# Low parts of weights and rotary products of a two-block model: from GpSimd to VectorE

## Chip, cores and metric

The kernel runs on one core of a Trainium2 chip. The metric is the device time of one execution in microseconds (us), the median of several runs. The engines are called as in the profile: PE is TensorE (PEld its weight loads), DVE VectorE, ACT ScalarE, POOL GpSimd, SP SyncE.

## What is computed

The reference runs two transformer blocks of two layers each on 512 tokens of 1024 features, in float32. The first block (differential attention, a recurrent branch, a gated feed-forward part) is not touched by the change. The second one is:

```python
def second_block(x, mem, positions, ...):
    for l in range(DEPTH):
        mix = hybrid_mixer(x, positions, w_in[l], conv_w[l], rel_bias[l], w_mix_out[l])
        x = layer_norm(ALPHA * x + mix, ln1_g[l], ln1_b[l])
        cross = memory_cross_attention(x, mem, w_mq[l], w_mkv[l], w_mo[l])
        x = layer_norm(ALPHA * x + cross, ln2_g[l], ln2_b[l])
        ff = squared_relu_mlp(x, w_ff1[l], w_ff2[l])
        x = layer_norm(ALPHA * x + ff, ln3_g[l], ln3_b[l])
    return x
```

`hybrid_mixer` projects x once and splits the result for three paths: a short gated convolution; an attention in which each query attends to the 128 keys that an indexer scores highest (8 small heads, a relu, a weighted sum, then a top-k); and an attention in chunks of 64 tokens over a band, with a relative bias. Queries and keys of the second path and of the indexer are turned by rotary tables:

```python
    rot = jnp.concatenate([x1 * cos - x2 * sin, x2 * cos + x1 * sin], axis=-1)
```

## The kernel before

Features lie on the partitions. Every large product is made of three float32r matmuls (`mm3`): high part of the weight by high part of x, high by low, low by high. A weight of 128 output features (128x1024 for all input features) is loaded by `weight` (L83): SP starts the load of `wraw` (L88), ACT rounds it to the high part `whi` (L90), and VectorE or, where `eng` says so, GpSimd subtracts that to get the low part `wlo` (L92). Each of the three tiles has three buffers, so the next weights are made while PE works on this one. A product over 512 tokens takes 24 matmuls.

```python
        (eng or nc.vector).tensor_sub(lo[:, :kt], raw[:, :kt], f(hi[:, :kt]))
```

`POOLW` (seven numbers) sets who makes the low parts in the second block's mixer: the first three numbers stand for the three weights of each pair of heads of the chunk attention (`C`), the fourth for the queries (`Q`), the last three for the convolution (`conv`). Before, the first and the third of each three are GpSimd's: 10 of them per layer, between weights that DVE makes.

`rope` (L643 to L654) turns a projection p: DVE swaps rows into `rt` (L650) and multiplies p by the cosines into `ru` (L651), `rt` is multiplied by the sines (L652), DVE adds the two (L653). It is called for the keys (two products of 64 rows each time), the indexer's queries and the queries.

`Norm.close` makes the last products before a norm over half the tokens at a time, and between them loads up to three weights of the next part ahead. The second one (`i == 1`) has its low part made by GpSimd. That happens at three places: before the first feed-forward products in both layers, and before the second layer's mixer.

The mixer's order is written in `STEPS2`: `H`, `I` input products, `i2`, `i1`, `i3` the indexer for three tiles of queries with 384, 256 and 512 keys (128x384, 128x256 and 128x512 sums called `isc`), `Q` queries, `C` and `A` chunk attention, `v` convolution, `d` attention to the chosen keys, `p` a part of the top-k. In the indexer (L876 to L888) PE makes the scores of a head into one of two banks `sc` (L880), ACT applies the relu into one of two buffers `p` (L882), DVE adds the weighted result to `isc` (L887 the first head, L884 the others). The top-k (L895 MAX8, L896 MATCH_REPLACE, L899 at its end) runs on DVE in pieces among the attentions. An attention adds its bias on DVE (L814), takes the exponential on ACT, the reciprocal on DVE (L817) and scales on ACT (L821); PE then transposes (L827) and multiplies.

The program is not run in the order in which it is written: a list scheduler of the framework sets, from its own costs, the order of each engine's queue. Each engine then works through its queue in order. A change of engine for one kind of operation so also changes the order of others.

Of the kernel before, what the change touches and what calls it, by code (L numbers as in the profile page):

```python
# [25 lines left out]
# columns of the first block's packed per-feature parameters  # L26
G_MIX, G_FFN, QG, KG, SUB, CW, CB, BRG, BIG, LRU, RECG, LAM = 0, 8, 16, 17, 18, 19, 35, 39, 43, 47, 51, 55
N_PAR1 = 59
# columns of the packed shape constants
# [5 lines left out]
# columns of the second block's packed per-feature parameters  # L35
# [11 lines left out]
def both_blocks(ctx: ExitStack, tc: tile.TileContext, xT, cst, par1, w1in, w1out, w1gu, w1dn, wgate,  # L47
# [6 lines left out]
    EARLY = 4  # tiles of features that the norms' first centre is taken from  # L54
# [7 lines left out]
    # ---- residual (features on partitions) and constants  # L62
# [4 lines left out]
    # the operand of most products: 8 tiles in two parts each  # L67
# [14 lines left out]
    # ---- building blocks  # L82
# [23 lines left out]
    def share(part):  # L106
        """who has the extra bank in a part of the program"""
        nonlocal extra
        extra = EXTRA[part]
# [18 lines left out]
    def rsqrt(pool, v, rows, n, between=()):  # L128
        """1/sqrt: y from half the exponent, then y (1 + a polynomial of v y^2 - 1) to the last bit"""
# [23 lines left out]
    def rnorm(pool, xs, a, b, rhs, n, eps):  # L153
        """1/sqrt(the sums of xs over the partitions, as rhs groups them, / n + eps), on every partition of a group"""
# [36 lines left out]
    def tables():  # L191
        """rope tables of the given positions"""
# [27 lines left out]
    # ================= first block  # L220
    WOUT = ((0, 4), (4, 8))  # what the mixer's output product sums over, group by group
    # weights of the second block's mixer whose low parts GpSimd makes
    POOLW = (1, 0, 1, 0, 1, 0, 1)
    # tiles of the output product over half the tokens at a time, at its end and its start
    MIXTAIL = 3
    MIXHEAD = 0
    # steps whose weights are scaled by VectorE
    BYDVE = ('A010', 'A201', 'A211')
    # the first input products of the second block's mixer
    HEAD = (2, 3, 0)  # L230
    # pairs of tiles that a norm writes as one
    MERGED = (2, 4)
    # the order of the tiles of queries for the choice of keys
    TOPK = (2, 3, 1)
    # the order of the second block's mixer: H I Q input products, i scores of the indexer, p a part of the choice of
    # keys, d attention to the chosen ones, C and A attention in chunks (pair, head, group of rows), v convolution
    STEPS2 = ('H', 'I', 'Q0', 'i2', 'Q2', 'i1', 'i3', 'Q1', 'C0', 'd0', 'A000', 'A001', 'C1', 'A011', 'A100', 'A010', 'A101', 'p', 'A110', 'A111', 'C2', 'v0', 'p', 'd3', 'p', 'p', 'A201', 'p', 'd2', 'v1', 'A200', 'p', 'd1', 'A211', 'p', 'A210')
    # the order of the first block's mixer: r recurrent branch, k q v of a head pair, a attention (pair, group of rows),
    # g gates, R their norm, w output product
# [3 lines left out]
    for l in range(2):  # L243
# [4 lines left out]
        with ExitStack() as lay:  # L248
# [7 lines left out]
            def prep(gain, a, b):  # L256
                """h times the gain, in two parts; the rows' scale comes after the product"""
# [32 lines left out]
            # lambda  # L290
# [9 lines left out]
            # q gain with the scores' scale, subln gain with 1 - lam_init, half the gates' biases  # L300
# [4 lines left out]
            # c = 8 log_sigmoid(L) = 8 (min(L, 0) - log1p(exp(-|L|)))  # L305
# [4 lines left out]
            # log1p(e) = 2 atanh(e / (2 + e)), e / (2 + e) <= 1/3  # L310
# [14 lines left out]
            with ExitStack() as mixer:  # L325
# [14 lines left out]
                def recurrent(i):  # L340
# [20 lines left out]
                    # sigmoid(z) = (1 + tanh(z / 2)) / 2  # L361
# [10 lines left out]
                    # y = c r; expm1(y) = tanh(y / 2) (exp(y) + 1); expm1(2 y) = expm1(y) (expm1(y) + 2)  # L372
# [16 lines left out]
                def rows(m, gain, spans, dst):  # L389
                    """queries or keys: normalized, turned, stacked in parts"""  # L390
# [33 lines left out]
                def values(hd):  # L424
                    # v, brought to tokens on partitions
# [18 lines left out]
                def attend1(hd, grp):  # L444
# [9 lines left out]
                    # the keys of the last tile are masked for the rows before it  # L454
# [3 lines left out]
                    for i in tiles:  # L458
# [36 lines left out]
                        # to keys on partitions  # L495
# [13 lines left out]
                    for j in range(kts):  # L509
                        # the first 16 rows see the first tile of keys only  # L510
                        e = g - 256 if j else 0
                        mm3(ps[:, e:g], vh[:, j], vl[:, j], ath[:, j, e:g], atl[:, j, e:g], j == 0, j == kts - 1)
# [710 lines left out]
```

## Time and profile before

| | |
|---|---|
| median of 3 runs | 2865.7 us (2865.55 to 2867.1) |
| span of the profiled execution | 2861.2 us |
| PE, DVE, ACT, POOL busy | 2781.5, 1736.3, 1227.4, 367.0 us |
| low parts on DVE, all weights | 437, mean 1238 ns |
| low parts on POOL | 23, mean 2433 ns |
| first block | 0 to about 1275 us |
| mixers of the second block | about 1280 to 1475 us and 2070 to 2270 us |

The profiled execution is one execution; its span runs from its first to its last instruction, and the runs' times lie 4.5 us above it at the median. Busy time is the time in which an engine had an instruction; for PE the ends of matmuls are modelled. A chain that ended last is followed back from the last instruction, at each step to what released it. In rows of the timeline the first number is the start in us from the span's start, the second the duration in us; in brackets stands how long the engine had been idle and whose work ended that.

### The profile page before, as it was taken

Reading aid. Unit: us, or ns where it says so; the run is one execution under the profiler, and the core shown is the slowest. Engines: PE = TensorE matmul, PEld = TensorE weight load, DVE = VectorE, ACT = ScalarE, POOL = GpSimd, SP = SyncE. Lnnn points to the kernel's source line nnn. Section 1 sums busy time; section 2 is a strip of 40 time slices with the busy share of each in tenths; the row PEclk is TensorE's granted clock in tenths of the full one; section 3 lists DMA queues with packets and bytes.
Section 4 is the critical chain, followed back from the end, with each engine's and each line's share of the span. In section 5 each row is a group of like instructions: output and inputs, shape, how many; then the busy total and the mean of one; then the engine's idle time right before and its main releaser. Section 6 shows DMA issues by size and latency. Waiting matters only on the chain.

```text
span 2861.2 us, 42993 instructions
## 1 busy us (share of the span) xinstructions
PE 2781.5 (97%) x16548; PEld 2422.5 (85%) x16548; DVE 1736.3 (61%) x3534; ACT 1227.4 (43%) x2174; POOL 367.0 (13%) x403
## 2 busy tenths in 40 slices
PE   8989999999999999999999999999999999999998
PEld 7989999999887888887889888888877898888887
DVE  7887434457888434458977573333789875633335
ACT  6665222235665222235665442332445754433323
POOL 0011000000110000002220031111322110311112
PEclk9999999999999999999999999999999999999999
DMA  4332332332333333336324123333264242233331
GB/s 146 89 79 85 90 89 85 94 89 92 99 85 100 95 92 94 94 95 166 112 82 140 59 81 97 96 96 96 70 155 132 75 136 72 60 106 95 96 96 64
DMA packets 96491, 277.18 MB, mean 97 GB/s; under 512 B 13344, under 2 KB 20000, under 8 KB 96288
## 3 DMA queue, kind: packets, MB, share of 16 engines
q1 hardware_dynamic: 96288, 274.45, 32.7%
q8 instruction: 131, 2.15, 0.3%
q14 instruction: 72, 0.59, 0.1%
HBM read 241.82 MB, written 2.10 MB: 85 GB/s over the span
## 4 chain that ended last, share of the span: by engine, by line
PE 87%; DVE 8%; issue 2%; ACT 2%; POOL 1%; DMA 1%; SPq 0%; ACTq 0%; DVEq 0%; POOLq 0%
PE mm L97 25%; PE mm L98 25%; PE mm L96 25%; PE av L96 1%; PE av L97 1%; PE av L98 1%; PE av L161 1%; DVE wlo L92 1%; PE bc L827 1%; PE av L712 1%; PE tr L827 1%; DVE sq L402 1%; PE bc L176 0%; PE sc L96 0%; PE sc L833 0%
## 5 line engine op out<-in xcount | busy, mean ns | idle before, releaser
L96 PE MATMUL mm<-xh_all,whi 128*128 128x512 f32 (+2 forms) x2752 | 926.0, 338 | 12.4 <-ACT xh_all L260 6.8
L97 PE MATMUL mm<-xl_all,whi 128*128 128x512 f32 (+2 forms) x2752 | 930.3, 339 | 1.4 <-DVE xl_all L745 0.8
L98 PE MATMUL mm<-xh_all,wlo 128*128 128x512 f32 (+2 forms) x2752 | 925.9, 337 | 0.0
L90 ACT CAST whi<-wraw 128x1024 fp32r<-128x1024 f32 (+2 forms) x460 | 465.4, 1013 | 1017.7 <-PE mm L97 823.9
L92 DVE TENSOR_TENSOR wlo<-wraw,whi 128x1024 fp32r<-128x1024 f32 (+2 forms) x437 | 540.7, 1238 | 233.7 <-ACT whi L90 231.7
L96 PEld LDWEIGHTS mm<-xh_all,whi 128*128 128x128 f32 x2752 | 518.8, 189 | 66.6 <-ACT xh_all L260 6.8
L97 PEld LDWEIGHTS mm<-xl_all,whi 128*128 128x128 f32 x2752 | 519.8, 189 | 54.5 <-DVE xl_all L745 1.8
L98 PEld LDWEIGHTS mm<-xh_all,wlo 128*128 128x128 f32 x2752 | 521.0, 189 | 49.8
L1106 POOL TENSOR_TENSOR r<-r 128x512 f32<-128x512 f32 (+1 forms) x70 | 101.9, 1456 | 531.6 <-ACT r L1105 531.6
L97 PE MATMUL mm<-yl,whi 128*128 128x264 f32 (+1 forms) x528 | 169.9, 322 | 0.1
L98 PE MATMUL mm<-yh,wlo 128*128 128x264 f32 (+1 forms) x528 | 169.5, 322 | 0.0
L96 PE MATMUL mm<-yh,whi 128*128 128x264 f32 (+1 forms) x528 | 168.5, 320 | 0.0
L673 DVE TENSOR_TENSOR hall<-hall,mm 128x512 f32<-128x512 f32 (+1 forms) x82 | 46.6, 568 | 145.9 <-PE mm L98 145.9
L593 DVE TENSOR_TENSOR su<-mm,rbc 128x264 f32<-128x264 f32 (+1 forms) x66 | 34.3, 519 | 139.8 <-PE mm L98 139.8
L602 DVE TENSOR_TENSOR hall<-hall,mm 128x264 f32<-128x264 f32 (+1 forms) x72 | 37.1, 515 | 120.6 <-PE mm L98 120.6
L97 PEld LDWEIGHTS mm<-yl,whi 128*128 128x128 f32 x528 | 99.2, 188 | 8.8 <-DVE yl L122 0.6
L96 PEld LDWEIGHTS mm<-yh,whi 128*128 128x128 f32 x528 | 99.0, 188 | 7.6
L98 PEld LDWEIGHTS mm<-yh,wlo 128*128 128x128 f32 x528 | 99.2, 188 | 7.3
L588 DVE TENSOR_TENSOR sg<-mm,rbc 128x264 f32<-128x264 f32 (+1 forms) x66 | 34.0, 517 | 103.2 <-PE mm L98 101.6
L671 DVE SCALAR_TENSOR_TENSOR hall<-hall,mm 128x512 f32<-128x512 f32 x32 | 22.0, 687 | 66.9 <-PE mm L98 66.8
L692 POOL TENSOR_TENSOR accq<-accq,nsq 128x512 f32<-128x512 f32 (+1 forms) x48 | 57.9, 1205 | 25.4 <-ACT nsq L690 24.0
L432 POOL MEMSET vh<- 128x128 f32 x8 | 1.6, 205 | 463.6 <-PE mm L98 414.8
(672 smaller groups left out, 5446.3 us busy)
## 6 DMA issues: line engine op xcount, KB each, us to landing
wraw<-w2f SPq DMA_DIRECT2D x128, 512.0 KB, 3.7
wraw<-w1gu SPq DMA_DIRECT2D x88, 512.0 KB, 3.6
wraw<-w2in SPq DMA_DIRECT2D x44, 512.0 KB, 3.9
wraw<-w1in SPq DMA_DIRECT2D x40, 512.0 KB, 3.7
wraw<-w2mkv SPq DMA_DIRECT2D x32, 512.0 KB, 3.8
wraw<-w1dn SPq DMA_DIRECT2D x32, 448.0 KB, 3.3
wraw<-w1out SPq DMA_DIRECT2D x32, 256.0 KB, 2.7
wraw<-w1dn SPq DMA_DIRECT2D x16, 512.0 KB, 3.5
```

Of the source, the lines that this page charges most:

```text
L90: nc.scalar.copy(hi[:, :kt], raw[:, :kt])
L92: (eng or nc.vector).tensor_sub(lo[:, :kt], raw[:, :kt], f(hi[:, :kt]))
L96: nc.tensor.matmul(ps, wh, xh, start=first, stop=False)
L97: nc.tensor.matmul(ps, wh, xl, start=False, stop=False)
L98: nc.tensor.matmul(ps, wl, xh, start=False, stop=last)
L588: nc.vector.tensor_mul(sg[:, a:b], p, r2[:, a:b])
L593: nc.vector.tensor_mul(su[:, a:b], p, r2[:, a:b])
L602: nc.vector.tensor_add(h[m][:, a:b], h[m][:, a:b], p)
L673: nc.vector.tensor_add(X(m, a, b), X(m, a, b), p)
L692: nc.gpsimd.tensor_add(self.accq[:, a:b], self.accq[:, a:b], sq[:, a:b])
L827: nc.tensor.transpose(ps[:, 128 * j:128 * j + 128], p[:, 128 * j:128 * j + 128], ident)
L1106: nc.gpsimd.tensor_mul(r[:, a:b], r[:, a:b], r[:, a:b])
```

## The change

Three edits: the seven numbers of `POOLW` become 0, the sine product in `rope` goes to VectorE, and `Norm.close` no longer names GpSimd for the second weight. Comments are taken out of the file too, with the line numbers kept. The core of the diff:

```diff
-    POOLW = (1, 0, 1, 0, 1, 0, 1)
+    POOLW = (0, 0, 0, 0, 0, 0, 0)
...
-                nc.gpsimd.tensor_mul(t[o:e, a:b], t[o:e, a:b], si[o:e, a:b])
+                nc.vector.tensor_mul(t[o:e, a:b], t[o:e, a:b], si[o:e, a:b])
...
-                        loaded[key] = weight(key[0](key[1]), eng=nc.gpsimd if i == 1 else None)
+                        loaded[key] = weight(key[0](key[1]))
```

In all, 23 low parts and 20 rotary products change their engine (10 and 10 per layer of the mixer, and 3 low parts in `Norm.close`). Four of the rotary products of a layer are 128x512, two 128x256 and four 64x256.

The order of the queues changes with it. On DVE, in the indexer of layer 0, the first score sum (`isc_13000` is that of `i2`) now has low parts and a rotary product around it:

```order
 L650 STREAM_SHUFFLE rt<-mm 128x512
+L652 TENSOR_TENSOR rt<-rt,ct 128x512
 L887 TENSOR_SCALAR isc_13000<-p,iw 128x384
+L92 TENSOR_TENSOR wlo<-wraw,whi 128x1024
 L884 SCALAR_TENSOR_TENSOR isc_13000<-p,iw,isc_13000 128x384 x2
+L92 TENSOR_TENSOR wlo<-wraw,whi 128x1024
 L122 TENSOR_TENSOR nl<-ru,nh 128x512
 L651 TENSOR_TENSOR ru<-mm,ct 128x512
```

One of the two low parts is new on DVE; the other, of the next weight, stood behind a swap of rows some places further on, where the low part of the weight after it, new on DVE too, stands now. The low half of the first rotated queries (L122) stands behind both.

Further on in DVE's queue, behind the last score sum of layer 0 (`isc_13001`, that of `i3`), among the first attention (`d0`, whose scores are added to `isc_12998`) and the top-k:

```order
 L896 MATCH_REPLACE isc_13000<-m_13843,isc_13000 128x384
 L817 RECIPROCAL st<-st 128x1
+L92 TENSOR_TENSOR wlo<-wraw,whi 128x1024
+L126 SCALAR_TENSOR_TENSOR nl<-mm,nh 128x512
+L122 TENSOR_TENSOR dal<-tr,dah 128x128
+L817 RECIPROCAL st<-st 128x1
+L814 ISA p,st<-sc,isc_12998 128x128
+L814 ISA st 128x1
 L895 MAX m_13846<-isc_13000 128x8
-L817 RECIPROCAL st<-st 128x1
+L92 TENSOR_TENSOR wlo<-wraw,whi 128x1024
+L122 TENSOR_TENSOR dal<-bc,dah 128x128
```

These are the next low parts after those three; between the two places, in the sums of `i1` and `i3`, there is none.

In `Norm.close` of layer 0, before the feed-forward products, DVE's queue read before:

```order
L148 SCALAR_TENSOR_TENSOR nwy<-nwu,nwy 128x4
L743 SCALAR_TENSOR_TENSOR hall<-hall,par_12982,bc 128x256 x2
L733 TENSOR_TENSOR hall<-hall,bc 128x2x256
L745 SCALAR_TENSOR_TENSOR xl_all<-hall,par_12982,xh_all 128x256
L673 TENSOR_TENSOR hall<-hall,mm 128x256
L745 SCALAR_TENSOR_TENSOR xl_all<-hall,par_12982,xh_all 128x256
```

and reads now:

```order
L148 SCALAR_TENSOR_TENSOR nwy<-nwu,nwy 128x4
L92 TENSOR_TENSOR wlo<-wraw,whi 128x1024
L743 SCALAR_TENSOR_TENSOR hall<-hall,par_12982,bc 128x256 x2
L733 TENSOR_TENSOR hall<-hall,bc 128x2x256
L673 TENSOR_TENSOR hall<-hall,mm 128x256
L745 SCALAR_TENSOR_TENSOR xl_all<-hall,par_12982,xh_all 128x256
```

The low part stands directly behind the last step of the reciprocal root (L148), ahead of the scaling of the features (L743), which reads that root after PE has broadcast it.

## Rows read from the trace of the kernel before

**Rows 1.** The page, parts 1 and 4: busy time, and the chain that ended last.

```profile
PE 2781.5 (97%) x16548; PEld 2422.5 (85%) x16548; DVE 1736.3 (61%) x3534; ACT 1227.4 (43%) x2174; POOL 367.0 (13%) x403
PE 87%; DVE 8%; issue 2%; ACT 2%; POOL 1%; DMA 1%; SPq 0%; ACTq 0%; DVEq 0%; POOLq 0%
```

**Rows 2.** Stretches: length, PE, PEld, DVE, ACT, POOL busy us (instructions), PEclk, DMA, GB/s.

```profile
1250.00:1300.00 50.00, 49.98 (x289) 43.60 (x289) 31.49 (x58) 16.31 (x26) 7.66 (x13) 1.00 0.38 105
1300.00:1350.00 50.00, 43.73 (x194) 33.11 (x193) 42.57 (x84) 25.45 (x53) 16.55 (x11) 1.00 0.60 157
1350.00:1400.00 50.00, 50.00 (x270) 40.94 (x269) 49.19 (x149) 32.84 (x82) 12.48 (x22) 1.00 0.60 165
1400.00:1450.00 50.00, 49.03 (x269) 41.37 (x268) 48.08 (x143) 36.39 (x78) 4.42 (x12) 1.00 0.21 66
2050.00:2100.00 50.00, 46.55 (x281) 40.99 (x280) 42.64 (x92) 25.48 (x49) 13.28 (x16) 0.97 0.36 97
```

**Rows 3.** Groups of POOL by shape: busy us, mean ns, idle us before them.

```profile
L92 POOL TENSOR_TENSOR wlo<-wraw,whi 128x1024 fp32r<-128x1024 f32 x23 | 56.0, 2433 | 36.5 <-ACT whi L90 36.4
...
L652 POOL TENSOR_TENSOR rt<-rt,ct 64x256 f32<-64x256 f32 x4 | 2.9, 737 | 19.8 <-DVE rt L650 15.1 <-DVE nwt L139 4.7
```

**Rows 4.** Timeline of POOL in the indexer of layer 0: start, duration, instruction.

```profile
1318.58 2.65 POOL L92 TENSOR_TENSOR wlo<-wraw,whi 128x1024 fp32r<-128x1024 f32 x1
...
1340.77 2.40 POOL L92 TENSOR_TENSOR wlo<-wraw,whi 128x1024 fp32r<-128x1024 f32 x1
```

**Rows 5.** DVE: timeline of layer 0's mixer; last, line L653 with min/median/max ns.

```profile
1306.92 1.21 DVE L92 TENSOR_TENSOR wlo<-wraw,whi 128x1024 fp32r<-128x1024 f32 x1
...
1315.92 0.62 DVE L884 SCALAR_TENSOR_TENSOR isc<-p,iw,isc 128x384 f32<-128x384 f32 x1 [2.59 <-ACT p L882]
...
1318.91 2.46 DVE L887 TENSOR_SCALAR isc<-p,iw 128x256 f32<-128x256 f32 x1
...
1321.92 0.46 DVE L884 SCALAR_TENSOR_TENSOR isc<-p,iw,isc 128x256 f32<-128x256 f32 x1
...
1322.78 1.04 DVE L884 SCALAR_TENSOR_TENSOR isc<-p,iw,isc 128x256 f32<-128x256 f32 x1
...
1326.87 2.63 DVE L884 SCALAR_TENSOR_TENSOR isc<-p,iw,isc 128x256 f32<-128x256 f32 x1
...
1341.36 2.89 DVE L92 TENSOR_TENSOR wlo<-wraw,whi 128x1024 fp32r<-128x1024 f32 x1
...
1414.21 1.50 DVE L993 TENSOR_SCALAR rt<-p,par 128x512 f32<-128x512 f32 x1
...
L653 DVE TENSOR_TENSOR ru<-ru,rt x16: 413/552/685, 1274.8 to 2118.1; 128x256 f32<-128x256 f32 x8, 128x512 f32<-128x512 f32 x8
```

**Rows 6.** Timeline of ACT: the relu behind the stretched score sum.

```profile
1321.47 0.38 ACT L882 ACTIVATE p<-sc 128x256 f32<-128x256 f32 x1 [2.60 <-DVE isc L887]
```

**Rows 7.** Timeline of PE: waits in the indexers of both layers.

```profile
1321.90 0.39 PE L880 MATMUL sc<-ik,iq 128*128 128x256 f32 x1 [1.73 <-ACT p L882]
...
1330.03 0.51 PE L880 MATMUL sc<-ik,iq 128*128 128x512 f32 x1 [1.66 <-ACT p L882]
...
1345.34 0.33 PE L827 MATMUL tr<-cs,p 128*128 128x128 f32 x1 [1.07 <-ACT p L821]
...
2113.72 0.39 PE L880 MATMUL sc<-ik,iq 128*128 128x256 f32 x1 [1.74 <-ACT p L882]
...
2121.85 0.50 PE L880 MATMUL sc<-ik,iq 128*128 128x512 f32 x1 [1.68 <-ACT p L882]
...
2136.95 0.35 PE L833 MATMUL sc<-dkh,dq 128*128 128x256 f32 x1 [1.14 <-issue]
```

**Rows 8.** Timeline of DVE: end of one choice of keys, and its first use.

```profile
1403.08 0.42 DVE L899 TENSOR_SCALAR isc<-isc 128x512 f32<-128x512 f32 x1
...
1419.13 0.68 DVE L814 CUSTOM_DVE_ANT_0 p<-sc,isc 128x512 f32<-128x512 f32 x1
```

**Rows 9.** Timeline of DVE: closing of a norm in layer 0.

```profile
1685.92 0.87 DVE L743 SCALAR_TENSOR_TENSOR hall<-hall,par,bc 128x256 f32<-128x256 f32 x2 [0.53 <-PE bc L722]
```

## Prediction

> **What bounds the kernel now.** I read the page first. TensorE (PE) is busy 2781.5 of 2861.2 us, VectorE (DVE) 1736.3 and GpSimd (POOL) 367.0; the chain that ended last lies 87% on PE, 8% on DVE and 1% on POOL [rows 1]. So only an edit that moves one of PE's few waits can move the end, and POOL's own time is worth almost nothing. Then I read the busy time by stretches of 50 us, because the averages hide the stage that the change touches [rows 2]: in 1300 to 1350 us, the indexer of layer 0 of the second block, PE works 43.73 of 50 us, the poorest stretch of this layer. In 1350 to 1400 and 1400 to 1450, where DVE picks the keys (top-k) among the attentions, PE is full, 50.00 and 49.03, and so is DVE, 49.19 and 48.08. There DVE has nothing left to hide new work under; whether PE minds is the question of this case.
>
> Next I read POOL's own lines [rows 3]: 23 low parts, 2433 ns each. Last I laid the three timelines of the indexer beside each other. On POOL, low parts begin at 1318.58 and 1340.77 and last 2.65 and 2.40 us [rows 4]. On DVE, the operation that starts just behind each of them stretches until POOL's has ended [rows 5]: the first score sum (L887) that starts at 1318.91 takes 2.46 us; an L884 takes 2.63 at 1326.87 and 0.46 at 1321.92; the low part that DVE itself makes takes 2.89 at 1341.36 and 1.21 at 1306.92; the convolution's L993 takes 1.50. ScalarE's next relu (L882) then waits 2.60 us for DVE to give back a buffer of `p` [rows 6], and PE's next score product waits 1.73 us for that relu [rows 7]. The same happens at 1330.03 (1.66 us) and, by a softmax whose reciprocal stands behind the stretched low part, at 1345.34 (1.07 us). Layer 1 repeats it: 1.74, 1.68 and 1.14 us [rows 7]. That is 4.46 us of PE's waits in layer 0 and 4.56 in layer 1.
>
> The Trainium skill, "SBUF — State Buffer", section "Who interferes with whom", says that a VectorE instruction with two SBUF inputs contends with a GpSimd instruction that reads SBUF, and that the later one fully blocks; the trace agrees, with 2.63 against 0.46 us for the same L884. By that rule alone every low part taken off POOL would pay, which is the faster rival below.
>
> **The change, part by part.**
>
> *Low parts of the mixer.* Ten weights per layer move from POOL to DVE. A DVE low part takes 1.21 us undisturbed [rows 5], so DVE gets 10 x 1.21 = 12.1 us per layer. The order of instructions tells where. Two of the ten, and the one between them that DVE made before too, stand ahead of the last two of the three score sums, about where DVE idles, 2.59 us before the L884 at 1315.92 for one [rows 5]; none stands inside those sums; the low part of the next weight comes only behind them.
>
> Inside the sums DVE loses the blocks of 1318.91 (2.46 less 0.46 is 2.0 us) and 1326.87 (2.63 less 0.46 is 2.2), and one by a rotary product of POOL at 1322.78 (1.04 less 0.46 is 0.6) [rows 5]. It gains one rotary product of 0.69. DVE so ends the sums about 4.1 us earlier. For PE the ends are 0 (the low part that now comes late holds PE as long as the blocks did) and 4.5 us per layer (all three waits go). I take half of the first two waits, (1.73 + 1.66)/2 = 1.7 us per layer: two low parts in front of the low half of the first rotated queries push those back, and PE must then wait for the low part behind the sums. **Indexer: 2 x -1.7 = -3.4 us.**
>
> Behind the sums DVE gets the other eight low parts (the first is the one that comes late), 8 x 1.21 = 9.7 us, and loses the blocks of 1341.36 (2.89 less 1.21) and 1414.21 (1.50 less at most 0.69, a product of the same size), 2.5 us: +7.2 us per layer in a stretch where it is 96 to 98% busy. Less the lead of 4.1 it ends top-k 3.1 us later. What covers this is the time between the end of a choice and its use: the choice for the last tile ends at 1403.08, its first scores are taken up at 1419.13, 16 us on [rows 8]. The other five POOL low parts of this stretch stretch no DVE operation that I found, so their removal gives nothing back. Ends for PE: 0 (the cover holds everything) and +3.1 per layer (softmax steps, which stand in DVE's queue behind the low parts, come late as a body). I take +1.0, nearer to the covered end. **Top-k stretch: 2 x +1.0 = +2.0 us.**
>
> *Rotary products.* Ten per layer come to DVE, four of 0.69 us and six of 0.42 (the longest and the shortest sum of the same shapes, L653 [rows 5]): 5.3 us. The four are in the account above or lie in DVE's idle time. The six stand in the head of the mixer, where the rotated keys are awaited: 6 x 0.42 = 2.5 us on DVE, beside which each of the two 64-row products that follow each other on POOL gets about 0.3 us shorter (0.74 us there [rows 3]). In layer 0 the head lies in a stretch where DVE is 31.49 us busy of 50 and PE 49.98 [rows 2]: hidden. In layer 1 it lies behind a norm (PE 46.55, DVE 42.64 of 50): ends -0.6 and +2.5, and I take **0**, since the chain is shorter and DVE has idle time there too. If this cover fails, it is the 2.5.
>
> *Closing of the norms.* At three places (two before the feed-forward products, one before layer 1) the second of the weights loaded ahead moves to DVE: +1.21 us each, in a chain of small DVE steps that PE waits for. In the new order it stands right behind the step (L148) after which DVE now idles 0.53 us for the broadcast by PE [rows 9]. So it costs 1.21 less 0.53, 0.7 at most, and nothing if the two sums that POOL stretches there get their time back. I take half, 0.35. **Closing: 3 x +0.35 = +1.05 us.**
>
> **Sum:** -3.4 + 2.0 + 0 + 1.05 = -0.35 us. The profiled span is 2861.2 us, the median of the runs 2865.7; I assume the 4.5 us around the span unchanged and add the difference to the median: **2865.4 us, no change that can be measured** (0.2%, 5.7 us, is about what a measurement of this kernel can tell from no change).
>
> **Rivals.**
>
> 1. *VectorE becomes the bound of the top-k stretch: slower.* DVE runs its queue in order. A low part that moves to its queue must wait for ScalarE's high part, and whatever stands behind it (score sums, softmax, top-k) waits too; on POOL such a wait held nobody up. If that eats the lead of 4.1 us, the full +7.2 us per layer reaches PE. With the indexer's 1.7 still gained this is 2 x (7.2 - 1.7) + 1.05 = +12.05, 2877.8 us; with the closing at its full price (2.1) and no gain in the indexer 2 x 7.2 + 2.1 = +16.5, 2882.2; with half of the lead kept, 2 x (5.15 - 1.7) + 1.05 = +7.95, 2873.7. The point from which it decides: DVE's lateness, 3.1 us in my sum, reaches what the softmax steps can bear; this, unlike the 16 us of the choices, the trace does not show. For it speaks that DVE is 96 to 98% busy there, against it that PE, with several weights in hand, works through (50.00 of 50). The Trainium skill, "Perfetto Trace Analysis", section "Optimizing Scalar/DVE Operations", leans this way: with VectorE saturated it may make sense to move work off to GpSimd, and the change does the opposite. The 49.19 us busy of 50 are such a saturated stretch. The same section doubts the gain between these two engines because they share a read port, so it settles nothing.
>
> 2. *The blocks were the price: faster.* All three PE waits per layer go, 4.46 + 4.56 = 9.0 us, the closing costs nothing and the shorter rotary chain gives 0.6 in layer 1: -9.6, 2856.1 us. For it: the chain POOL to DVE to ScalarE to PE is plain in four rows [rows 4 to 7]. Against it: DVE's work rises by 12.1 + 5.3 = 17.4 us per layer, against some 7.3 us of blocks that I count (2.0 + 2.2 + 0.6 + 2.5); so the wait may return elsewhere, and the late low part is one place for it.
>
> 3. *POOL was off the path and DVE has room: nothing moves.* Both effects stay below 1 us a layer, -1 to +2; this falls in with my forecast's band.
>
> **How the numbers follow.** No measurable change: 0.42 (forecast and rival 3). Slower by over 0.2%: 0.33, since the new work on DVE outweighs the blocks and lands where DVE is full. Faster by over 0.2%: 0.25, since the waits that the blocks cause are real but only 9 us in all. The range reaches from the faster rival's 2856.1 to a little above the slower one's 2877.8, which leaves the worst prices out: 2856 to 2878. The forecast's own band is 2860.0 to 2871.4.
>
> **What would show it right or wrong.** In the profile of the changed kernel no L92 and no L652 runs on POOL, and DVE's busy time rises by about 23 x 1.21 = 28 us and 11 us of products less 2 x 7.3 = 15 us of blocks, so by some 24. L884 keeps to 0.46 to 0.74 us throughout the indexer, and PE's waits of 1.73 and 1.66 us before L880 shrink or go, while one for a low part (L98, on `wlo`) appears behind the last score product, about 1333 to 1340. In 1350 to 1450 PE stays above 98.5 of 100 us: if it falls by several us there, with DVE at 50 of 50, the first rival is right. If 1300 to 1350 gains over 4 us and 1350 to 1450 loses none, the second is. The prediction is wrong in its reasons, whatever the time, if the last choice of keys ends earlier than before, or if PE waits at the head of layer 1 or in the closings more than 1 us longer than now.

## The result, and the profile after

The changed kernel takes **2883.88 us** (2879.87 to 2887.97, four runs) against 2865.62 before (2865.53 to 2867.1, four runs): the ratio is **1.0058**, with an interval of 1.0044 to 1.0072. It is slower by 0.6%, and the time lies outside the range of 2856 to 2878. The profiled execution has a span of 2886.2 us against 2861.2, 25.0 more; the spans of the four runs go from 2878.1 to 2886.2, with mean granted clocks of TensorE from 0.991 down to 0.987 (0.995 in the profiled execution of the kernel before).

Busy time and the chain that ended last, from the page of the changed kernel:

```profile
PE 2800.7 (97%) x16548; PEld 2438.6 (84%) x16548; DVE 1746.8 (61%) x3577; ACT 1229.9 (43%) x2174; POOL 292.8 (10%) x360
PE 84%; DVE 10%; issue 2%; ACT 1%; DMA 1%; SPq 1%; POOL 1%; DVEq 0%; ACTq 0%; POOLq 0%
```

The edit does what it says: POOL loses 74 us and 43 instructions, which DVE has more [rows 1]. DVE's busy time grows by 10.5 us only. PE makes the same 16548 matmuls and is busy 19.2 us longer; its idle time grows by 5.8. So the loss sits mostly inside PE's busy time: the matmuls came slower, by clock or by an empty pipeline.

The 25.0 us of the profiled execution lie, stage by stage (from the first score product of a layer's indexer and the norms' step L148): first block, which no edit touches, +2.6; mixer of layer 0 +10.6; closing in layer 0, with the feed-forward part, +1.6; second norm and head of layer 1 +1.8; mixer of layer 1 +5.5; last closing +3.0. In the first block the granted clock was lower (0.93 instead of 0.97 at 200 to 300 us). It was lower in other stages too, where the kernel before had 1.00 (columns as in [rows 2]; the clock is the third number from the end):

```profile
1700.00:1750.00 50.00, 47.83 (x280) 41.97 (x279) 31.11 (x58) 29.49 (x56) 11.29 (x11) 0.97 0.27 85
2100.00:2150.00 50.00, 44.85 (x184) 34.77 (x183) 38.19 (x79) 23.71 (x47) 0.44 (x3) 0.92 0.58 141
2500.00:2550.00 50.00, 46.98 (x278) 41.91 (x278) 32.57 (x61) 29.01 (x56) 13.45 (x13) 0.93 0.28 86
```

A clock of 0.93 over 50 us is 3.5 us of full speed, at most, so the clock can have a part in the shares of the closings and of layer 1; how large it is no run shows by itself.

Stretches of the changed kernel, to be read against [rows 2] (length, PE, PEld, DVE, ACT, POOL busy us, granted clock, DMA, GB/s). The last line is layer 1:

```profile
1300.00:1350.00 50.00, 44.02 (x189) 33.88 (x188) 39.36 (x83) 25.67 (x52) 0.43 (x3) 0.97 0.62 156
1350.00:1400.00 50.00, 49.75 (x259) 39.99 (x258) 48.05 (x142) 31.55 (x76) 2.70 (x16) 1.00 0.52 146
1400.00:1450.00 50.00, 46.55 (x229) 37.40 (x227) 46.78 (x139) 29.56 (x63) 1.55 (x10) 0.93 0.20 60
1424.00:1428.00 4.00, 2.44 (x12) 1.45 (x11) 3.99 (x15) 3.33 (x8) 0.00 (x0) 1.00 0.00 0
1432.00:1434.00 2.00, 1.32 (x5) 0.66 (x3) 1.29 (x5) 1.56 (x5) 0.00 (x0) 0.50 0.00 0
1430.00:1440.00 10.00, 8.64 (x35) 7.18 (x34) 8.32 (x28) 7.33 (x17) 0.00 (x0) 0.66 0.14 38
2230.00:2240.00 10.00, 6.40 (x29) 3.56 (x28) 9.69 (x35) 8.92 (x19) 0.00 (x0) 1.00 0.00 0
```

and the kernel before at the place where the changed one is slow:

```profile
1430.00:1440.00 10.00, 10.00 (x59) 8.98 (x58) 9.54 (x28) 8.70 (x20) 0.14 (x1) 1.00 0.20 67
```

From 1350 to 1450 us PE is busy 49.75 + 46.55 = 96.3 of 100 us, not over 98.5 as I wrote. But DVE has not filled up: 48.05 and 46.78, less than before. A stage that loses on PE while DVE works less is not bound by DVE's amount of work; something makes the two take turns.

DVE's timeline in layer 0 shows what the edit was hoped to do, and one thing more (start, duration, instruction, idle time before it):

```profile
1322.02 0.35 DVE L887 TENSOR_SCALAR isc<-p,iw 128x256 f32<-128x256 f32 x1
...
1324.31 0.48 DVE L884 SCALAR_TENSOR_TENSOR isc<-p,iw,isc 128x256 f32<-128x256 f32 x1 [1.29 <-ACT p L882]
...
1412.03 0.42 DVE L899 TENSOR_SCALAR isc<-isc 128x512 f32<-128x512 f32 x1
...
1423.99 0.68 DVE L814 CUSTOM_DVE_ANT_0 p<-sc,isc 128x512 f32<-128x512 f32 x1
...
1436.31 1.20 DVE L92 TENSOR_TENSOR wlo<-wraw,whi 128x1024 fp32r<-128x1024 f32 x1
```

The score sums are undisturbed (0.35 and 0.48 us instead of 2.46 and 2.63 [rows 5]). The last choice of keys still ends 12 us before its use (1412.03 to 1423.99; 16 us before [rows 8]). The low part at 1436.31 is the next weight's. ACT had its high part ready at 1424.47, but six softmax adds of 512 keys (L814) stand ahead of it in DVE's queue.

PE's timeline, indexer and attention to the chosen keys (`d3`), of the changed kernel:

```profile
1324.33 0.39 PE L880 MATMUL sc<-ik,iq 128*128 128x256 f32 x1 [1.40 <-ACT p L882]
...
1342.80 0.56 PE L98 MATMUL mm<-xh_all,wlo 128*128 128x512 f32 x1 [1.05 <-DVE wlo L92]
...
1424.73 0.50 PE L833 MATMUL sc<-dkh,dq 128*128 128x512 f32 x1 [0.19 <-DVE st L814]
1425.07 0.40 PE L834 MATMUL sc<-dkl,dq 128*128 128x512 f32 x1
1426.84 0.50 PE L833 MATMUL sc<-dkh,dq 128*128 128x512 f32 x1 [1.37 <-DVE st L814]
...
1433.45 0.69 PE L96 MATMUL av<-dah,dvvh 128*128 128x384 f32 x1 [0.68 <-ACT dah L121]
...
1435.20 0.52 PE L96 MATMUL av<-dah,dvvh 128*128 128x384 f32 x1
1435.52 0.52 PE L97 MATMUL av<-dal,dvvh 128*128 128x384 f32 x1
```

and of the kernel before, from the same score product (the third of `d3`, the attention of the tile with 512 keys) to the same `av` product:

```profile
1419.87 0.50 PE L833 MATMUL sc<-dkh,dq 128*128 128x512 f32 x1 [0.97 <-DVE st L814]
1420.21 0.39 PE L834 MATMUL sc<-dkl,dq 128*128 128x512 f32 x1
1420.44 0.39 PE L97 MATMUL mm<-xl_all,whi 128*128 128x512 f32 x1
1420.67 0.40 PE L98 MATMUL mm<-xh_all,wlo 128*128 128x512 f32 x1
...
1428.16 0.40 PE L96 MATMUL av<-dah,dvvh 128*128 128x384 f32 x1
```

Here is the largest part of the loss. Both kernels take about the same time from the third score product to the first `av` product: 8.29 us before, 8.72 after. But before, PE did 17 matmuls of a weight's product in that time, 17 x 0.234 = 4.0 us of work; after, it did none. PE's queue, in the order of instructions, before:

```
L833 sc, L834 | L97 L98 L96 L97 L98 L96 L97 mm | L833 sc, L834 | L827 tr x4 | L833 sc, L834 | L98 L96 L97 mm | L833 sc, L834 | L98 ...
```

and after:

```
L833 sc, L834 | L833 sc | L827 tr x4 | L834 | L833 sc, L834 | L833 sc, L834 | L827 bc x4 | L833 sc, L834 | L827 tr x4 | L96 av
```

With nothing in between, PE goes at the pace of the softmax steps of DVE and ACT (it waits 1.37 us for L814 and 0.68 for L121), and the weight's product is done elsewhere: 4.0 + 8.72 - 8.29 = 4.4 us lost. Layer 1 has the same counts, 17 and none, and 7.81 and 8.21 us: 4.4 again. In layer 0 there is a second loss: the granted clock is at 0.50 (1.2 GHz) from about 1432 to 1439, after PE was 2.44 of 4 us busy at 1424, and `av` products follow each other at 0.32 us instead of 0.18. A mean of 0.66 over 1430 to 1440 is 3.4 us of full speed, at most. In layer 1 the same stretch (2230 to 2240) is as empty, 6.40 of 10 us, but the clock stays at 1.00, and the loss from `d3` to the output product is 5.45 us instead of 7.55 (the table below).

How much later each place comes than before, counted from the first score product of the indexer (L880) of its layer, layer 0 / layer 1, in us. The columns headed by other kernels are of the third group of experiments:

| place | after | new order, no edit | edits, old order | part of the edits, old order |
|---|---|---|---|---|
| first softmax add of `d0` | -2.36 / -2.22 | -2.41 / -1.95 | -2.07 / -2.32 | -2.05 / -2.35 |
| first softmax add of `d3` | +2.30 / -0.15 | +2.08 / +1.28 | +2.70 / +1.96 | -2.61 / -2.50 |
| first softmax add of `d2` | +7.51 / +1.92 | +7.43 / +5.51 | +2.69 / +1.97 | -2.61 / -2.49 |
| first product of the output | +9.85 / +5.30 | +10.07 / +8.85 | +2.67 / +1.95 | -2.60 / -2.17 |

A place can also come earlier because PE's new order has put other products behind it. PE from the first score product to the first softmax add of `d0`, layer 0 and layer 1 (length, PE busy us (matmuls), granted clock, DMA, GB/s), in the kernel before:

```profile
1297.67:1340.44 42.77, 37.60 (x164) 1.00 0.59 157
2089.05:2132.57 43.52, 37.83 (x164) 1.00 0.63 159
```

and in the changed one:

```profile
1300.24:1340.65 40.41, 35.87 (x157) 1.00 0.57 142
2105.53:2146.83 41.30, 37.27 (x153) 0.92 0.58 145
```

The changed kernel has 7 and 11 matmuls of 512 columns fewer there, 1.6 and 2.6 us of work at 0.234 each. So of its -2.36 and -2.22 us at `d0` only some 0.7 in layer 0 is time gained, and nothing in layer 1, where the clock was at 0.92. With all queues in the old order the count is 164 in both layers, and the two right-hand columns are time gained or lost.

### The profile page after: what moved, and what is told of

Read it like the earlier page. It is cut to its first block, busy times and chain, and to the rows that moved or that the text cites. A ratio compares the mean times of both kernels' runs of the same rounds, so it can differ in the third digit from the quotient of the medians.

```text
span 2886.2 us, 42950 instructions
## 1 busy us (share of the span) xinstructions
PE 2800.7 (97%) x16548; PEld 2438.6 (84%) x16548; DVE 1746.8 (61%) x3577; ACT 1229.9 (43%) x2174; POOL 292.8 (10%) x360
## 4 chain that ended last, share of the span: by engine, by line
PE 84%; DVE 10%; issue 2%; ACT 1%; DMA 1%; SPq 1%; POOL 1%; DVEq 0%; ACTq 0%; POOLq 0%
PE mm L97 25%; PE mm L98 25%; PE mm L96 25%; DVE wlo L92 1%; PE av L96 1%; PE av L97 1%; PE av L98 1%; PE av L161 1%; DVE isc L896 1%; PE av L712 1%; DVE m L895 1%; PE bc L827 1%; PE tr L827 1%; DVE sq L402 1%; SPq L845 0%
## 5 line engine op out<-in xcount | busy, mean ns | idle before, releaser
L92 DVE TENSOR_TENSOR wlo<-wraw,whi 128x1024 fp32r<-128x1024 f32 (+2 forms) x460 | 562.1, 1222 | 238.0 <-ACT whi L90 235.8
L816 ACT ACTIVATE p<-p,st 128x128 f32<-128x128 f32 (+3 forms) x96 | 53.5, 559 | 9.3 <-DVE st L814 8.8
```

The costliest lines, as they stand in the source:

```text
L816: nc.scalar.activation(p[:, :nk], p[:, :nk], AF.Exp, bias=st[:, 0:1], scale=-1.0, accum_out=st[:, 1:2])
```

## The experiments

The first theory was my rival 1: the work that came to DVE outweighs the blocks that went (theory D in the expectations). Its rival: the list scheduler makes another order out of the edits, and the order costs, whoever does the work (rival or theory O). All ratios are to the kernel before, run on the same chip beside them; its medians there were 2864.83, 2865.28, 2867.51 and 2867.3 us.

**Parts of the change, each alone.** The scheduler sets an order of its own for each of these kernels.

`e1_mixer_low_parts`, the mixer's low parts alone:

```diff
-    POOLW = (1, 0, 1, 0, 1, 0, 1)
+    POOLW = (0, 0, 0, 0, 0, 0, 0)
```

> The kernel before with only the ten low parts per layer of the second block's mixer moved to VectorE; rotary products and the closings stay on GpSimd. Theory D (VectorE's queue in the top-k stretch is what was lost: new work there makes the choices of keys and the softmax steps late, PE runs dry and its clock falls after): this edit alone carries most of the loss, 2873 to 2884 us against 2865.6, with PE waits at the first scores of the attention over 512 chosen keys and a granted clock under 1 just behind them. Rival C (the closings of the norms carry it): under 2870. Rival O (any reordering by the scheduler costs as much): slower, but no more than each of the two other edits alone.

Measured: 2884.23 us, 1.0068 (1.0056 to 1.0081). This part alone gives the whole loss, at the top of theory D's range; that no part costs more than another, as I had put rival O, is wrong.

`e2_rotary`, the rotary products alone:

```diff
-                nc.gpsimd.tensor_mul(t[o:e, a:b], t[o:e, a:b], si[o:e, a:b])
+                nc.vector.tensor_mul(t[o:e, a:b], t[o:e, a:b], si[o:e, a:b])
```

> The kernel before with only the rotary sine products moved to VectorE. Theory D: they end before the top-k stretch, the indexer loses one block of 0.6 us per layer and gets as much work; 2863 to 2868 us, no change. Rival O (reordering alone): slower by over 4 us, over 2870.

Measured: 2872.69 us, 1.0028 (1.0017 to 1.0039), as rival O had it. I had put it at 0. The mixers lose 5.2 and 2.8 us, and not where the products stand. DVE's and POOL's timelines in layer 0:

```profile
1383.57 0.29 DVE L814 CUSTOM_DVE_ANT_0 p<-sc,bt 128x128 f32<-128x128 f32 x1 [2.10 <-POOL bt L967]
```

```profile
1383.39 0.14 POOL L967 MEMSET bt<- 64x64 f32 x1 [4.78 <-DMA bt<-rel]
```

In the new order the load of a chunk's bias (`bt`) comes late, POOL clears its corner late, and DVE waits 2.10 us for that; in the kernel before DVE never waits for `bt` there. I take this for the order's work, far from the edited line; that the wait makes the whole loss is not shown.

`e3_closings`, the three low parts in the closings alone:

```diff
-                        loaded[key] = weight(key[0](key[1]), eng=nc.gpsimd if i == 1 else None)
+                        loaded[key] = weight(key[0](key[1]))
```

> The kernel before with only the three low parts in the closings of the norms moved to VectorE. Theory D: +1 to +5 us by the trace of the changed kernel (its later stretches fall behind by 1.3, 1.5 and 3.0 us there), 2867 to 2871 us. Rival C (closings carry the loss): +8 or more, over 2873.

Measured: 2870.56 us, 1.0017 (1.0008 to 1.0027): small, within theory D's range, but more than the 1.05 us of my sum. In its profile the first closing stands at +2.05, the stage with the second at -0.3 and the last at +1.4, and the mixer of layer 1, of which nothing was moved, at +2.2.

`e9_first_pair` moves only the low parts of the first pair of `C` (at L940 and L951 `... and pr > 0 and nc.gpsimd`), and `e4_first_pair_and_rotary` these and the rotary products, so that the blocks in the score sums go and little new work comes behind them:

> The kernel before with only the first pair's two moved low parts (C0) on VectorE, all else as before. Theory D: these stand in VectorE's idle time of the indexer and free it of one block; 2860 to 2866 us. Rival O: slower by 4 or more, over 2869, by a wait for a transfer or a queue elsewhere.

> The kernel before with the rotary products and only the first pair's two moved low parts (C0) on VectorE; the other eight per layer and the closings stay on GpSimd. Theory D: the indexer keeps what it gained (2 to 3 us per layer, as in the changed kernel), and the top-k stretch is not loaded: 2859 to 2864 us, faster than both kernels. Rival O: slower than before, over 2868.

Measured: 2875.99 us, 1.004 (1.0025 to 1.0055), and 2874.2 us, 1.0028 (1.0018 to 1.0038). Four low parts of the two layers on DVE cost 0.4%, and with the rotary products on top no more than that. Both lie in rival O's range, outside theory D's. Amounts of work don't add like this.

`e7_late_eight` moves the other eight low parts of each layer (`pr == 0 and` in the same two lines, `eng=None` for the convolution's):

> The kernel before with only the eight later low parts per layer on VectorE (second and third pair and the convolution); the first pair's two, the rotary products and the closings stay on GpSimd. Theory D: this is where the loss is, 2874 to 2884 us, with TensorE waiting at the first scores over 512 chosen keys and a lower granted clock there. Rival O: about as much as the rotary products alone cost, 2870 to 2875, with the waits in other places.

Measured: 2886.02 us, 1.007 (1.0053 to 1.0087), as slow as all of them and above theory D's range. The first four alone and the other sixteen alone lose 0.4% and 0.7%, together (e1) 0.7%.

**Less work for DVE.** Two kernels run 14 rounds of the top-k instead of 16, so they choose 112 keys instead of 128; one is the changed kernel, one the kernel before:

```diff
-                    for r in range(16):
+                    for r in range(14):
...
-                        if r % 4 == 3:
+                        if r in (3, 7, 10, 13):
```

> The changed kernel with 14 instead of 16 rounds of maximum and replace per choice of keys (it chooses 112 keys instead of 128, so this part of the computation is cut). That takes about 6.0 us per layer off VectorE in the top-k stretch (two rounds of 1.25, 1.0 and 0.75 us for the three tiles), nearly the 7.2 that the change put there. Theory D (VectorE is full there and its lateness reaches TensorE and then its clock): most of the loss goes, 2864 to 2871 us, and the difference to the kernel before with 14 rounds falls to under 8. Rival O (the order of the queues costs, whatever VectorE has to do): 2876 to 2884 us, the difference stays at 14 to 20.

> The kernel before with 14 instead of 16 rounds of maximum and replace per choice of keys (112 keys instead of 128). Both theories: TensorE is full in the top-k stretch of the kernel before and the choices have 16 us of slack, so 2858 to 2866 us, next to nothing gained; if it gains over 6, the kernel before was bound by VectorE there too.

Measured: 2880.26 us, 1.0055 (1.004 to 1.007), and 2877.64 us, 1.0045 (1.003 to 1.0059). The first time lies in theory O's range, the second in neither's, and the difference of 2.6 us is theory D's. Taking DVE's work away gave the changed kernel next to nothing back (1.0055 instead of 1.0058), and the kernel *before* with less work became 0.45% **slower**. No engine has more to do in it, and it loses 12 us; what is left to lose them is the order. It is no clean test of DVE's load, since each of the two kernels has an order of its own, but it sent me to look at the order by itself.

**Work and order apart.** The next kernels are built twice in one file: the first build, with edits `FIRST`, gives the scheduler's order; the second, with edits `THEN`, adds a dependence without a semaphore from each instruction to the one ahead of it on its engine in that order:

```diff
+            if order is not None:
+                last = {}
+                traced = {i.name: i for i in nc.cur_bb.bb.instructions}
+                for name in order:
+                    i = traced.get(name)
...
+                    before = last.get(str(i.engine))
+                    if before is not None:
+                        tc.add_manual_dep(i, before, mybir.DependencyInfo(mybir.DependencyClass.NoSync, mybir.DependencyReason.DATA), reason="order")
+                    last[str(i.engine)] = name
```

Each engine then keeps the order of the first build, and an instruction that changes its engine stands, on the new one, where its turn was.

`p1_change_in_old_order`: the whole change, in the order of the kernel before.

> All three edits, but every engine's queue keeps the order of the kernel before: the program is first scheduled with the work on GpSimd, then built with it on VectorE with an edge from each instruction to the one ahead of it in its queue; a moved operation stands in VectorE's queue where the first schedule started it. So VectorE does the same work as in the changed kernel, and no other queue is in another order. Theory O (the order that the scheduler makes after the edits costs): 2860 to 2868 us, next to the kernel before. Theory D (VectorE's added 17 us per layer cost, wherever they stand): 2874 to 2886 us.

`p2_old_engines_in_new_order`: no edit, in the order of the changed kernel.

> No edit: GpSimd makes the low parts and rotary products as before, but every engine's queue keeps the order of the changed kernel. VectorE does the work of the kernel before, GpSimd's low parts block it as before. Theory O: 2874 to 2886 us, as slow as the changed kernel. Theory D: 2862 to 2870 us.

Measured: the change in the old order 2871.67 us, **1.0015** (1.0006 to 1.0024), between the ranges of the two theories; the old engines in the new order 2885.3 us, **1.0059** (1.0046 to 1.0073), as theory O had it. The traces show that the orders were kept: in the first kernel all 16548 matmuls of PE and all 2174 instructions of ACT come in the order of the kernel before, in the second in that of the changed kernel, from which PE's order before differs at 1543 places. The order alone, with no work moved, costs what the change costs. The moved work alone costs a quarter of it, in the old order; in the new order it adds nothing (1.0058 against 1.0059). Stretches of the kernel without an edit in the new order:

```profile
1350.00:1400.00 50.00, 49.65 (x261) 40.26 (x260) 45.50 (x137) 31.54 (x78) 12.13 (x20) 1.00 0.54 148
1400.00:1450.00 50.00, 46.52 (x229) 37.38 (x228) 44.03 (x135) 29.68 (x63) 6.29 (x12) 0.93 0.21 62
1430.00:1440.00 10.00, 9.05 (x36) 7.76 (x36) 8.27 (x27) 6.51 (x14) 0.00 (x0) 0.66 0.01 3
```

and PE around `d3` in it:

```profile
1425.49 0.50 PE L833 MATMUL sc<-dkh,dq 128*128 128x512 f32 x1 [1.52 <-DVE st L814]
...
1432.17 0.69 PE L96 MATMUL av<-dah,dvvh 128*128 128x384 f32 x1 [0.68 <-ACT dah L121]
```

The loss of PE (46.52 against 46.55 us busy), the clock of 0.66 and the missing weight product are those of the changed kernel, while DVE is busy 44.03 of 50 us. The change in the old order, over the same stretches:

```profile
1300.00:1350.00 50.00, 45.74 (x201) 34.52 (x199) 41.79 (x91) 26.54 (x55) 0.72 (x3) 1.00 0.61 159
1350.00:1400.00 50.00, 48.13 (x251) 38.09 (x251) 49.39 (x141) 31.83 (x77) 2.87 (x16) 1.00 0.60 161
1400.00:1450.00 50.00, 48.12 (x259) 39.86 (x260) 48.49 (x147) 33.66 (x75) 2.07 (x13) 1.00 0.23 72
```

Here the indexer gains (45.74 against 43.73 [rows 2]) and the top-k stretch loses 1.87 and 0.91, with DVE at 49.39 of 50: rival 1's mechanism, at its true size. From `d0` to `d3` of layer 0 PE waits there 1.4 us for DVE's `cal` (L122) and 1.2 us for its softmax adds (L814), and for neither in the kernel before. In the table this is -2.07 to +2.67 in layer 0 and -2.32 to +1.95 in layer 1, so +4.7 and +4.3 us.

`p4_indexer_in_old_order`: old order; only the rotary products and the low parts of the first two pairs of `C` move to DVE, the other six of each layer and the closings stay POOL's.

```diff
+FIRST = {}; THEN = {'rope': 1, 'pairs': 2}
-                    w = weight(win(7 + 3 * pr), eng=POOLW[0] and nc.gpsimd)
+                    w = weight(win(7 + 3 * pr), eng=POOLW[0] and pr >= ON_DVE.get('pairs', 0) and nc.gpsimd)
```

(and so at L951)

> In the order of the kernel before: the rotary products and the low parts of the first two pairs (C0, C1: the four per layer that fall into the indexer, three of which block VectorE there) go to VectorE; the other six per layer and the closings stay on GpSimd. If the blocks cost what the waits before the scores showed (4.5 us per layer) and VectorE is not loaded further on, 2857 to 2863 us, faster than both kernels. If VectorE's added work of some 10 us per layer weighs more than the blocks: 2866 to 2874.

Measured: **2862.01 us, 0.9983** (0.9974 to 0.9992), faster than both kernels. That is less than the 0.2% that I had called measurable, but it rests on 11 runs against 20. Its stretches, and two of PE's waits in the indexer:

```profile
1300.00:1350.00 50.00, 46.34 (x205) 35.32 (x204) 41.79 (x95) 27.69 (x57) 3.14 (x4) 1.00 0.62 163
1350.00:1400.00 50.00, 50.00 (x270) 40.93 (x269) 49.18 (x147) 32.64 (x81) 12.64 (x22) 1.00 0.62 166
1400.00:1450.00 50.00, 49.05 (x269) 41.34 (x268) 48.05 (x143) 36.66 (x79) 4.11 (x12) 1.00 0.21 64
```

```profile
1324.26 0.39 PE L880 MATMUL sc<-ik,iq 128*128 128x256 f32 x1 [0.74 <-ACT p L882]
...
1330.37 0.51 PE L880 MATMUL sc<-ik,iq 128*128 128x512 f32 x1 [0.64 <-ACT p L882]
```

The waits of 1.73 and 1.66 us [rows 7] are down to 0.74 and 0.64, and the 2.6 and 2.5 us gained at `d3` are still there, but for 0.3 in layer 1, at the output product (-2.60 and -2.17 in the table); the mixer's new low parts on DVE all stand ahead of them.

**One queue at a time.** All edits, with only PE's queue (`p6_old_tensor_queue`) or only DVE's (`p7_old_vector_queue`) held to the old order:

```diff
-                    if i is None:
+                    if i is None or KEPT not in str(i.engine):
```

> All three edits; only TensorE's queue keeps the order of the kernel before, the other queues are scheduled anew around it. If the loss is that TensorE's queue has no products of weights left between the scores and the softmax steps over 512 chosen keys, the time falls to 2868 to 2874 us, as with all queues kept (2871.7), and the waits there are short. If it is VectorE's or another queue's order: 2878 to 2888 us.

> All three edits; only VectorE's queue keeps the order of the kernel before, the other queues are scheduled anew around it. If VectorE's order is what costs (the choices of keys stand behind other work and end late), 2868 to 2874 us. If it is TensorE's queue: 2878 to 2888 us, with the same waits at the scores over 512 chosen keys.

Measured: 2881.09 us, 1.005 (1.0035 to 1.0065), and 2887.93 us, 1.0073 (1.0056 to 1.009). Neither brings the time back. PE in the first and then in the second waits elsewhere instead:

```profile
1338.61 0.80 PE L98 MATMUL mm<-xh_all,wlo 128*128 128x512 f32 x1 [2.55 <-DVE wlo L92]
```

```profile
1328.22 0.58 PE L880 MATMUL sc<-ik,iq 128*128 128x256 f32 x1 [3.57 <-ACT p L882]
```

The queues hang together: an old order on one against a new one on the others is a third order. Which single queue costs is therefore still open. The first kernel does bear on `d3`, though: PE's queue is the old one there, so the 17 matmuls stand between the softmax steps again. Its places come at -4.02 / -2.55 us (`d0`), +4.49 / +2.98 (`d3`), +4.42 / +4.80 (`d2`) and +7.78 / +5.06 (output product). From `d3` to `d2` it loses nothing in layer 0 and 1.8 us in layer 1, where the unedited kernel in the new order loses 5.4 and 4.2; it loses 8.5 and 5.5 us between `d0` and `d3` instead. So with the matmuls there `d3` is covered again in layer 0, and the loss stands elsewhere.

## Why the prediction was wrong

**The step that failed** is "Top-k stretch: 2 x +1.0 = +2.0 us". From `d0` to the output product the changed kernel loses 2.36 + 9.85 = 12.2 us in layer 0 and 2.22 + 5.30 = 7.5 in layer 1, 19.7 together; 4.2 of that are the 18 matmuls that stood ahead of `d0` before, the rest is lost. I read the new order at three places and priced only DVE's work in it; that the order of PE's own queue would change far from any edited line, and take the weight's product out from between the softmax steps of `d3`, was in no term of the sum. The kernel in the new order with no edit, whose PE queue is the same, comes 12.5 and 10.8 us later there, so this is shown to be the order. That the missing 17 matmuls make 4.4 us of it per layer, and the clock up to 3.4 more in layer 0, is read from the rows; neither was tried by itself (`p6_old_tensor_queue` puts the matmuls back, with a third order around them). The rows do hold one comparison for the clock: from the first softmax add of `d3` to the output product the loss is 7.55 us in the changed kernel's layer 0 and 7.99 and 7.57 in the unedited kernel in the new order, three places where the clock fell, and 5.45 in the one where it did not.

**The same step without the new order** was too small as well: +4.7 and +4.3 us per layer in the old order, above the upper bound of +3.1 that I had. I had counted the lead twice: the indexer's term credits PE with 1.7 us of it, and the top-k term takes all 4.1 off again. In the run the lead at `d0` is 2.1 to 2.3 us, and PE has had it by then. What the eight low parts bring is then the gross 7.2, of which 4.7 and 4.3 reached PE; the covers that I named held 2.5 to 2.9 us. This is my reckoning: no run moves these eight alone in the old order.

**Rival 1** has the right sign, and 2882.2 us, its worst price, is near the measured time, but not by its mechanism. Its sign in the profile was DVE at 50 of 50 while PE falls; PE fell, and DVE was at 46.78. Its mechanism alone costs 9.0 us in the top-k stretches, against 4.4 gained in the indexers. In the old order its closest price was "half of the lead kept", +7.95; that kernel's profile stands at +8.9 and its median at +4.2.

**Indexer, 2 x -1.7: right in kind and too small in the old order, not reached in the new one.** In the old order PE is 2.07 and 2.32 us earlier at `d0` with the same work done; in the changed kernel the gain is some 0.7 and nothing. L884 keeps to 0.46 to 0.75, as forecast; a wait for a low part appears behind the sums as forecast, at 1342.80, and is 1.05 us. Of the waits that I had priced, the 1.14 us in layer 1 stands in its row as "issue": the profile names no releaser for it.

**Rotary and head, 0.** In the old order the second norm and head of layer 1 come to +0.6 us with all edits made. Alone, with the order that it brings, this edit costs 0.28%.

**Closings, 3 x +0.35: the size of the moved work, without its order.** In the old order the stretches between the two halves' L148 grow by 0.26, 0.47 and 0.26 us, 1.0 together against 1.05; in the changed kernel by 1.0, 1.2 and 2.2. In layer 0, from the norm's step L148 to the scaling L743 the new order too gives my size (1.17 us before, 1.71 after, +0.54 against 0.7 at most):

```profile
1697.92 0.65 DVE L148 SCALAR_TENSOR_TENSOR nwy<-nwu,nwy 128x4 f32<-128x4 f32 x1
1698.49 1.21 DVE L92 TENSOR_TENSOR wlo<-wraw,whi 128x1024 fp32r<-128x1024 f32 x1
1699.63 0.86 DVE L743 SCALAR_TENSOR_TENSOR hall<-hall,par,bc 128x256 f32<-128x256 f32 x2
...
1701.85 1.23 DVE L92 TENSOR_TENSOR wlo<-wraw,whi 128x1024 fp32r<-128x1024 f32 x1
```

But the low part that DVE made before too also moved forward, ahead of the lows of x (L745), and the stretch of two halves, from this L148 to the second half's L743, went from 14.43 to 15.42 us; in the old order it takes 14.69. The order again; in the last closing the lower clock (0.93 at 2500 to 2550) lies on top.

**DVE's busy time** rose by 10.5 us, not by 24. By the traces the low parts brought 21.4 us net (L92, 540.7 to 562.1) and the sine products 10.5; the score sums (L884, L887) gave back 14.9 where I had counted 9.6, and L993 2.2.

**The chances.** Slower had 0.33. The list of rivals had no case for "the scheduler's new order is worse, whatever the work", though I knew that a scheduler set it; with it, the upper end of 2878 might not have stood.

## What to carry to other kernels

Under a list scheduler an edit of engines is two changes, another distribution of work and another program order; the second can be the larger one, as it was here, and it strikes in queues that the edit does not name. Price them apart: hold every queue to the old order and measure the edit, then measure the new order without the edit; here +0.15% and +0.59%, and the part of the edit worth having was 0.17% faster in the old order. In the order itself, count on the bounding engine how many independent matmuls stand between the dependent steps of each softmax chain, since that is the cover that vanished here without any instruction being added. That cover is not all: with PE's queue alone back in the old order the loss was still 0.5%.

## What the runs showed of the hardware that I had not expected

TensorE's granted clock fell to 0.50, its lower level of 1.2 GHz, from about 1432 to 1439 us, after PE had been busy only 2.44 of 4 us at 1424; at 2230 to 2240 the same chain of products, 6.40 of 10 us busy, left it at 1.00, and in the unedited kernel in the new order it fell in both layers (`av` products 0.52 us long at 2240.66 too). So the same thin chain of this order was followed by a fall in three of four places. Part of the difference between runs of one kernel goes with the clock: the changed kernel's four spans follow their mean clocks, 2878.1 us at 0.991 and 2886.2 at 0.987, 2.0 us for each 0.001. The clock does not explain the loss away: at a mean clock of 0.991 the unedited kernel in the new order took 2883.5 us and the kernel before, on the same chip, 2868.1 to 2870.7; at 0.993 they took 2880.4 and 2865.5 to 2866.8. So 13 to 15 us remain at an equal clock, and the rest of its 18 goes with a lower one.
